# Layer 1, 64 dense tokens of block 1: high and low part of the acts as one operand of 128 columns in the output products

## The chip, the cores and the metric

One NeuronCore of a Trainium2 chip runs the whole program. The metric is the device time of one execution in microseconds, the median of some runs. A profile is one more execution, taken with the hardware profiler. Engines: PE (matrix products), DVE (VectorE), ACT (ScalarE), POOL (GpSimd, which issues the gathers) and SP (which issues the other transfers, in order).

## The reference, cut to what matters

A decoder trunk of two layers over 512 tokens of 1024 features. Each layer ends in a PEER mixer: eight heads choose 16 of 16,384 experts for each token, an expert being one row of `u_tab` and one of `v_tab`.

```python
        u = u_tab[e]
        a = jax.nn.gelu(jnp.einsum('pd,phkd->phk', xb, u).astype(jnp.float32), approximate=False)
        return jnp.einsum('phk,phkd->pd', g * a, v_tab[e].astype(jnp.float32)).astype(xb.dtype)
```

Here `e` are a token's 128 expert numbers, `g` their softmax weights, and the sum over them goes into the residual stream with a gate (`g2`).

## The kernel before, in words

The mixer is computed in two ways at once. For some tokens it is *sparse*: the chosen rows are gathered from DRAM, 128 rows of 1024 at a time (`gather_back`), and VectorE makes the dot products and the weighted sums. In layer 1 these are the 128 tokens of block 0 and the first 64 of block 1: 384 gathers, of which 96 come ahead of the dense steps. For the others it is *dense* (`dense`): all 16,384 experts are gone through in 128 steps of 128 experts, with a table of weights that is zero where a token did not choose an expert. In layer 1 these are 320 tokens, `T = 320`: the last 64 of block 1 (`LO[1] = 64`), and blocks 2 and 3, which in `dense` are b = 0, 1 and 2.

A dense step i has two products. The *act products* (L658) multiply a tile `u` of 128 experts with the 320 tokens' inputs into the PSUM tile `pa`; GELU and the weights `wg` make `g`, 128 experts by 320 tokens. The *output products* (L695) multiply `g`, as the stationary operand, with a tile `v` of 128 experts by 1024 features, and add into six PSUM banks `Y[b][h]`, three token blocks by two halves of 512 features. Operands are split into a high and a low part (float32r), `XH`, `XL` for `u` and `v`, `WH`, `WL` for `g`: ScalarE casts the high part (L246), VectorE subtracts for the low part (L247). A product is three matmuls: high by high, high by low, low by high. The first 28 steps' acts are made ahead (`NA = 28`, tile `ahead`), so steps 0 to 27 have output products only. In the program, step i+1's act products come ahead of step i's output products.

The order on each engine is set by the tile framework's scheduler, from priorities and its own estimate of durations; gathers' VectorE work is tied to steps by a list:

```python
PACE = [[1.5] * 28 + [2.5] * 100, [1.5] * 28 + [2.46] * 100]
```

So layer 1 takes 1.5 gathered tiles a step in steps 0 to 27 and 2.46 a step after. `u` and `v` share three buffers of 512 KB, gathered tiles four, and `wg` comes in ten loads of 256 KB for 16 steps, from the table that the kernel wrote to DRAM as `wd`.

After the last step `dense_end` multiplies `Y` with the gate row, adds the residual tiles `XD` and calls `final`, which normalizes and stores `out`. Its tiles (`XD`, `gate`, the norm's row `fg`, `fo`) are in a pool of their own, `fe`, opened when the dense pools are closed in the program's text; its memory is what those pools leave free, or free up. The tile `ahead` with its pad holds 28 x 320 x 4 + 768 = 36,608 bytes a partition until step 27 has read it. The `end` of the sparse part sums the two halves of the last gathered sum `y` (`go` brings the upper 64 partitions down), and does the same for its tokens with `gt`, `gx` and `gfg`.

Of the kernel before, what the change touches and what calls it, by code (L numbers as in the profile page):

```python
# [10 lines left out]
F32 = mybir.dt.float32  # L11
F32R = mybir.dt.float32r
# [4 lines left out]
ALU = mybir.AluOpType  # L17
# [3 lines left out]
P = 128  # L21
D = 1024
# [8 lines left out]
NK = 128  # L31
# [6 lines left out]
NBD = 3  # L38
# [3 lines left out]
LO = (0, 64)  # L42
# [9 lines left out]
def kernel(ctx, tc, x, c_col, pos, mod_w, mod_b, norm_g, w_in, w_gl, w_g2, b_g2, gla_ng, gla_wo,  # L52
                      kv_mod_w, kv_mod_b, kv_ng, kv_w, swa_wq, sinks, swa_wo, peer_wq, subk, peer_u, peer_v,
                      u_t, v_t, fin_g, out):
    nc = tc.nc
# [135 lines left out]
    def gated_add(env, X, half, y, gate, rows=slice(0, P)):  # L191
        t = env.tmp.tile([P, 512], F32, tag=env.t2k, name="ga")[rows]
        nc.vector.tensor_tensor(t, y[rows], gate[rows], op=ALU.mult)
        nc.vector.tensor_tensor(X[rows, ts(half, 512)], X[rows, ts(half, 512)], t, op=ALU.add)
# [50 lines left out]
    def split_rows(src, H, L, eng=nc.vector):  # L245
        cast = nc.scalar.copy(H, src)  # L246
        eng.tensor_tensor(L, src, H.bitcast(F32), op=ALU.subtract)  # L247
        return cast
# [351 lines left out]
    def dense(l, yps):  # L600
        Y = []
        first = []
        lastg = []
        outs = []
        lo = LO[l]
        T, G0 = TD - lo, lo // TG
# [5 lines left out]
        with tc.tile_pool(name="dna", bufs=1, reuse_waits="tile") as da, \  # L612
# [34 lines left out]
            def halves():  # L647
                return [dp.tile([P, D], F32R, tag=t, name=t, bufs=3) for t in ("XH", "XL")]

            def act(i, out, bank="pa"):  # L650
                u = dp.tile([P, KT, P], F32, tag="uv", name="u", bufs=3)
                nc.sync.dma_start(u, u_t[l, i])
                UH, UL = (t.rearrange("p (k t) -> p k t", t=P) for t in halves())
                split_rows(u, UH, UL)
                pa = psa.tile([P, 512], F32, tag=bank, name="pa")
                for n, (uu, hh) in enumerate(((UH, hH), (UH, hL), (UL, hH))):
                    for kt in range(KT):
                        nc.tensor.matmul(pa[:, :T], uu[:, kt, :], hh[:, kt, lo:], start=n + kt == 0,  # L658
                                         stop=n == 2 and kt == KT - 1)
                nc.scalar.activation(out, pa[:, :T], AF.Gelu)  # L660
# [8 lines left out]
            def stage1(i, wg):  # L669
                g = dp.tile([P, T], F32, tag="g", name="g")  # L670
                if i < NA:
                    src = ahead[:, i, :]
                else:
                    src = g
                    act(i, g)
                v = dp.tile([P, D], F32, tag="uv", name="v", bufs=3)
                nc.sync.dma_start(v, v_t[l, i])
                VH, VL = halves()
                split_rows(v, VH, VL)
                first.append(nc.vector.scalar_tensor_tensor(  # L680
                    g.rearrange("p (g t) -> p g t", t=TG), src.rearrange("p (g t) -> p g t", t=TG), 1.0 / GSC,
                    wg[:, :, ts(i % SL, TG)], op0=ALU.mult, op1=ALU.mult))
                WH = dp.tile([P, T], F32R, tag="WH", name="WH", bufs=2)
                WL = dp.tile([P, T], F32R, tag="WL", name="WL", bufs=2)
                lastg[:] = [split_rows(g, WH, WL)]
                return VH, VL, WH, WL

            def rows(b):
                return slice(0, P if b else P - lo)

            def stage2(i, VH, VL, WH, WL, blocks=range(NBD)):
                for b in blocks:
                    for a, vv in ((WH, VH), (WH, VL), (WL, VH)):
                        for h in range(2):
                            mm = nc.tensor.matmul(Y[b][h][rows(b), :], a[:, max(b * P - lo, 0):(b + 1) * P - lo], vv[:, ts(h, 512)],  # L695
                                                  start=i == 0 and a is WH and vv is VH,
                                                  stop=i == NK - 1 and a is WL)
                outs.append(mm)

            cur = slot(ds_)  # L700
# [16 lines left out]
            with tc.tile_pool(name="dnw", bufs=1, reuse_waits="tile") as dw:  # L717
                for k in range(parts):
                    slot_part(0, cur, k)
                Y += [[yps.tile([P, 512], F32, tag=f"y{2 * b + h}", name="Y") for h in range(2)] for b in range(NBD)]  # L720
                work = stage1(0, cur)
                for i in range(NK):
                    m, k = divmod(i, SL)
                    if k == 0 and i + SL < NK:
                        nxt = slot((dw, ds_)[m % 2])
                    if k < parts and i + SL < NK + k:
                        slot_part(m + 1, nxt, k)
                    if k == SL - 1:
                        cur = nxt
                    then = stage1(i + 1, cur) if i + 1 < NK else None  # L730
                    if i < NK - 2:
                        stage2(i, *work)
                    elif i == NK - 2:
                        for w, blocks in ((work, (0, 1)), (then, (0, 1)), (work, (2,)), (then, (2,))):
                            stage2(i + (w is then), *w, blocks)
                    work = then
        return Y, first, outs, lastg[0]

    def dense_end(fp, l, Y, X, after):
        gate = fp.tile([P, D], F32, tag="gate", name="gate")  # L740
        nc.sync.dma_start(gate, grow[l].partition_broadcast(P))
        for b in range(NBD):
            nc.sync.dma_start(X[b][:P if b else P - LO[l], :], xs[b + 1][0 if b else LO[l]:P, :])
        env = Env()
        env.tmp, env.t2k = fp, "t2k"
        for b in range(NBD):
            for h in range(2):
                gated_add(env, X[b], h, Y[b][h], gate[:, ts(h, 512)], slice(0, P if b else P - LO[l]))
            after(b)

    def preload_sqrt(pool, after):
# [241 lines left out]
    def swa_d(Y, yctx, mod, Ak, Bk, A, B, A4, B4, rbase, hT0, after, lastg):  # L993
        with ExitStack() as stack, tc.tile_pool(name="sd", bufs=1, reuse_waits="tile") as sp, \
# [34 lines left out]
            def after_add(b):  # L1029
                with tc.issue_after(first.ins):  # L1030
                    modulate_T(env, XD[b], (Ak, Bk, hk[b]), (A, B, hq[b]))

            dense_end(sp, 0, Y, XD, after_add)
            yctx.close()
            sps = stack.enter_context(tc.tile_pool(name="sdps", bufs=1, space=PSUM, reuse_waits="tile"))
# [153 lines left out]
    def ypool():  # L1189
        return tc.tile_pool(name="dnps", bufs=1, space=PSUM, reuse_waits="tile")  # L1190
# [5 lines left out]
    with prio(D0):  # L1196
        Y, at, outs, lastg = dense(0, yctx.enter_context(ypool()))
# [12 lines left out]
    with prio(D1):  # L1210
        Y, at, outs, lastg = dense(1, ctx.enter_context(ypool()))
        with prio(GG):
            gather_back(1, at, outs, *gs[1])
        with tc.tile_pool(name="fe", bufs=1, reuse_waits="tile") as fe:
            XD = xd_tiles(fe)
            fg = fe.tile([P, D], F32, tag="fg", name="fg")
            nc.sync.dma_start(fg, fin_g.partition_broadcast(P))
            env = Env()
            env.small = fe

            def final(b):
                o = fe.tile([P, D], F32, tag="fo", name="fo", bufs=2)
                lo = 0 if b else LO[1]
                q = slice(0, P - lo)
                r = rstd_of(env, XD[b][q, :], D, o[q, :], q)
                for h in range(2):
                    half = ts(h, 512)
                    nc.vector.scalar_tensor_tensor(o[q, half], XD[b][q, half], r, fg[q, half], op0=ALU.mult,
                                                   op1=ALU.mult)
                    nc.sync.dma_start(out[(b + 1) * P + lo:(b + 2) * P, half], o[q, half])  # L1230

            preload_sqrt(fe, lastg)
            dense_end(fe, 1, Y, XD, final)
# [67 lines left out]
```

## Time and profile before

| | us |
|---|---|
| median of 3 runs | 3237.35 (3230.11 to 3239.7) |
| the profiled execution's own time | 3229.43 |
| its span, first to last instruction | 3227.7 |
| PE, DVE, ACT busy | 2986.4, 2505.4, 1251.1 |
| layer 1's output products, first to last | 2312.5 to 3209.5 |

The span lies within the execution's time. Busy times are sums over the whole span, in which stages of different kinds follow each other; what a stage waits for is read in its own stretch. A PE row's length covers a matmul's whole way through the engine, so matmuls overlap in the rows: their pace is the distance between starts.

### The profile page before, as it was taken

The numbers are of one execution on the slowest core, as the hardware profiler recorded it, in microseconds if no ns is written. First come the engines' busy times: TensorE is split into PE (matmuls) and PEld (weight loads), VectorE is DVE, ScalarE is ACT, GpSimd is POOL, SyncE is SP. The second block draws the span as 40 slices with busy tenths as digits, with TensorE's granted clock in tenths as the row PEclk, the third lists the DMA queues.
The fourth block names the chain that finished last, engine by engine and source line by source line (L and its number), as shares of the span: only waits on it lengthen the run. The fifth ranks groups of instructions, "written<-read, shape, count | busy, mean of one in ns | idle before, by whom it ended". The sixth has DMA issues, their size and how long they took to land.

```text
span 3227.7 us, 45681 instructions
## 1 busy us (share of the span) xinstructions
PE 2986.4 (93%) x16674; PEld 2527.4 (78%) x16674; DVE 2505.4 (78%) x4879; ACT 1251.1 (39%) x1985; POOL 791.8 (25%) x669
## 2 busy tenths in 40 slices
PE   5999885999999999999999968789899999999997
PEld 4776685997999988999876535589678888878886
DVE  6865689978778777877653778889897877777888
ACT  3523323543333333333673332335433333433333
POOL 0000000025333433433000143320143333343332
PEclk9999998999999999999999979989899999999999
DMA  7678664889989999998634578877899899899987
GB/s 233 225 260 275 208 227 152 291 304 331 325 305 338 322 330 333 325 322 287 226 105 144 183 261 302 275 267 258 305 350 342 314 323 322 311 344 327 315 310 235
DMA packets 278970, 904.78 MB, mean 280 GB/s; under 512 B 29828, under 2 KB 75268, under 8 KB 273112
## 3 DMA queue, kind: packets, MB, share of 16 engines
q1 hardware_dynamic: 186584, 566.28, 49.8%
q0 software_dynamic: 92160, 335.59, 30.1%
q8 instruction: 130, 2.13, 0.3%
q14 instruction: 96, 0.79, 0.1%
HBM read 848.23 MB, written 52.96 MB: 279 GB/s over the span
## 4 chain that ended last, share of the span: by engine, by line
PE 58%; DMA 14%; DVE 12%; issue 10%; POOL 3%; ACT 2%; SPq 1%; POOLq 0%; DVEq 0%; ACTq 0%
PE Y L695 22%; PE pa L658 21%; PE ps_mm L545 4%; POOL gu L830 3%; DMA w<-in_peer_wq 3%; DMA u<-in_u_t 2%; DMA w<-in_mod_w 2%; PE pm L643 2%; DVE XL L247 2%; PE ps_m L1058 1%; DVE og L635 1%; DMA wg<-wd 1%; DMA gu<-in_peer_u,ei 1%; DVE gu L861 1%; DVE gacc L134 1%
## 5 line engine op out<-in xcount | busy, mean ns | idle before, releaser
L830 POOL DMA_INDIRECT gu<-in_peer_u,ei x256 | 324.2, 1266 | 1630.4 <-DVE gu L861 821.0
L247 DVE TENSOR_TENSOR XL<-u,XH 128x1024 fp32r<-128x1024 f32 x256 | 313.1, 1224 | 229.6 <-ACT XH L246 135.0
L695 PE MATMUL Y<-XH,WH 128*128 128x512 f32 (+1 forms) x1536 | 480.3, 393 | 11.4 <-ACT WH L246 11.4
L695 PE MATMUL Y<-XH,WL 128*128 128x512 f32 (+1 forms) x1536 | 477.3, 392 | 2.0 <-DVE WL L247 2.0
L695 PE MATMUL Y<-XL,WH 128*128 128x512 f32 (+1 forms) x1536 | 478.2, 392 | 0.1
L246 ACT CAST XH<-u 128x1024 fp32r<-128x1024 f32 x256 | 268.8, 1051 | 466.5 <-PE pa L658 233.1
L830 POOL DMA_INDIRECT gu<-in_peer_v,ei x256 | 315.9, 1234 | 517.1 <-DVE yg L873 458.3
L658 PE MATMUL pa<-hH,XH 128*128 128x384 f32 (+1 forms) x2048 | 380.6, 327 | 14.2 <-ACT g L660 12.4
L658 PE MATMUL pa<-hL,XH 128*128 128x384 f32 (+1 forms) x2048 | 377.8, 324 | 0.0
L658 PE MATMUL pa<-hH,XL 128*128 128x384 f32 (+1 forms) x2048 | 375.7, 323 | 2.2 <-DVE XL L247 2.2
L246 ACT CAST XH<-v 128x1024 fp32r<-128x1024 f32 x256 | 268.9, 1050 | 278.1 <-PE Y L695 240.2
L247 DVE TENSOR_TENSOR XL<-v,XH 128x1024 fp32r<-128x1024 f32 x256 | 312.8, 1222 | 73.5 <-ACT XH L246 72.0
L658 PEld LDWEIGHTS pa<-hH,XH 128*128 128x128 f32 x2048 | 340.5, 189 | 35.8 <-ACT g L660 18.0
L861 DVE SCALAR_TENSOR_TENSOR gu<-gu,htg 128x1024 f32<-128x1024 f32 x256 | 309.5, 1221 | 62.9 <-DMA gu<-in_peer_u,ei 62.5
L873 DVE SCALAR_TENSOR_TENSOR yg<-gu,a,yg 128x1024 f32<-128x1024 f32 x254 | 325.5, 1281 | 30.4 <-DMA gu<-in_peer_v,ei 28.9
L658 PEld LDWEIGHTS pa<-hL,XH 128*128 128x128 f32 x2048 | 337.8, 189 | 1.6 <-issue 0.8
L658 PEld LDWEIGHTS pa<-hH,XL 128*128 128x128 f32 x2048 | 335.3, 188 | 3.3 <-DVE XL L247 3.0
L695 PEld LDWEIGHTS Y<-XH,WL 128*128 128x128 f32 (+1 forms) x1536 | 275.0, 179 | 79.1 <-DVE WL L247 2.7
L695 PEld LDWEIGHTS Y<-XL,WH 128*128 128x128 f32 (+1 forms) x1536 | 275.3, 179 | 77.8 <-DVE XL L247 0.5
L695 PEld LDWEIGHTS Y<-XH,WH 128*128 128x128 f32 (+1 forms) x1536 | 274.1, 180 | 67.8 <-ACT WH L246 12.0
L246 ACT CAST WH<-g 128x384 fp32r<-128x384 f32 (+1 forms) x256 | 124.7, 487 | 456.8 <-DVE g L680 335.0
L545 PE MATMUL ps_mm<-hTd,w 128*128 128x128 f32 x1792 | 236.3, 291 | 32.1 <-DMA w<-in_peer_wq 27.0
(342 smaller groups left out, 3880.9 us busy)
## 6 DMA issues: line engine op xcount, KB each, us to landing
u<-in_u_t SPq DMA_DIRECT2D x256, 512.0 KB
v<-in_v_t SPq DMA_DIRECT2D x256, 512.0 KB
w<-in_peer_wq SPq DMA_DIRECT2D x128, 512.0 KB
w<-in_mod_w SPq DMA_DIRECT2D x96, 512.0 KB
wd<-wt SPq DMA_DIRECT2D x44, 1024.0 KB
wg<-wd SPq DMA_DIRECT2D x176, 256.0 KB
w<-in_gla_wo SPq DMA_DIRECT2D x32, 512.0 KB
w<-in_swa_wo SPq DMA_DIRECT2D x32, 512.0 KB
```

Of the source, the lines that this page charges most:

```text
L134: nc.vector.scalar_tensor_tensor(acc, w(kt), cs[:, kt:kt + 1], acc, op0=ALU.mult, op1=ALU.add)
L246: cast = nc.scalar.copy(H, src)
L247: eng.tensor_tensor(L, src, H.bitcast(F32), op=ALU.subtract)
L545: mm = nc.tensor.matmul(pq[:, ts(q, P)], w[:, kt, :], hT[:, kt, :], start=kt == 0, stop=kt == KT - 1)
L635: nc.vector.tensor_tensor(og[:, n], o2, wide(gn), op=ALU.mult)
L643: nc.tensor.matmul(pm[:, t, :], o1[:, u, :, w], og[:, n, u, :, w], start=n == 0, stop=n == 1)
L658: nc.tensor.matmul(pa[:, :T], uu[:, kt, :], hh[:, kt, lo:], start=n + kt == 0, stop=n == 2 and kt == KT - 1)
L695: mm = nc.tensor.matmul(Y[b][h][rows(b), :], a[:, max(b * P - lo, 0):(b + 1) * P - lo], vv[:, ts(h, 512)], start=i == 0 and a is WH and vv ...
L830: nc.gpsimd.indirect_dma_start(out=u, out_offset=None, in_=table, in_offset=bass.IndirectOffsetOnAxis(ap=e[:, i:i + 1], axis=0))
L861: nc.vector.scalar_tensor_tensor(u, u, 1.0, h, op0=ALU.mult, op1=ALU.mult, accum_out=a[:, i:i + 1])
L873: nc.vector.scalar_tensor_tensor(y, u, a[:, i:i + 1], y, op0=ALU.mult, op1=ALU.add)
L1058: nc.tensor.matmul(pqs[b], hTs[b][:, kt, :], w(kt), start=kt == 0, stop=kt == KT - 1)
```

## The change

Layer 1's block b = 0 has 64 tokens only. The high and low part of `g` now lie in one tile `W2` of 640 columns: 64 columns of low part of block 0, then 320 columns of high part, then the low part of the other two blocks. Its first 128 columns are block 0's low and high part side by side, and they are one stationary operand: with `VH` and with `VL`, two terms instead of three. The bank `Y[0][h]` then holds 64 rows of the low part's products and 64 rows of the high part's, which `dense_end` must add: it multiplies the whole bank with the gate into a tile `both`, has the upper 64 rows brought down by a transfer to a tile `low`, and adds both to `XD`. The blocks end in the order 1, 0, 2. In layer 0 (`LO = 0`) the tile is laid out anew, and the work is the same.

```diff
@@
-                WH = dp.tile([P, T], F32R, tag="WH", name="WH", bufs=2)
-                WL = dp.tile([P, T], F32R, tag="WL", name="WL", bufs=2)
-                lastg[:] = [split_rows(g, WH, WL)]
-                return VH, VL, WH, WL
-
-            def rows(b):
-                return slice(0, P if b else P - lo)
-
-            def stage2(i, VH, VL, WH, WL, blocks=range(NBD)):
+                W2 = dp.tile([P, 2 * T], F32R, tag="W2", name="W2", bufs=2)
+                n = T % P
+                H = W2[:, n:n + T]
+                lastg[:] = [nc.scalar.copy(H, g)]
+                for c in (slice(0, n), slice(n, T)):
+                    if c.stop > c.start:
+                        L = W2[:, 0:n] if n and not c.start else W2[:, n + T:]
+                        nc.vector.tensor_tensor(L, g[:, c], H[:, c].bitcast(F32), op=ALU.subtract)
+                return VH, VL, W2
+
+            def stage2(i, VH, VL, W2, blocks=range(NBD)):
+
                 for b in blocks:
-                    for a, vv in ((WH, VH), (WH, VL), (WL, VH)):
+                    if b or not lo:
+                        c = b * P - lo
+                        H, L = W2[:, T % P + c:][:, :P], W2[:, T + c:][:, :P]
+                        terms = (H, VH), (H, VL), (L, VH)
+                    else:
+                        both = W2[:, 0:P]
+                        terms = (both, VH), (both, VL)
+                    for n, (a, vv) in enumerate(terms):
                         for h in range(2):
-                            mm = nc.tensor.matmul(Y[b][h][rows(b), :], a[:, max(b * P - lo, 0):(b + 1) * P - lo], vv[:, ts(h, 512)],
-                                                  start=i == 0 and a is WH and vv is VH,
-                                                  stop=i == NK - 1 and a is WL)
+                            mm = nc.tensor.matmul(Y[b][h], a, vv[:, ts(h, 512)], start=i == 0 and n == 0,
+                                                  stop=i == NK - 1 and n == len(terms) - 1)
                 outs.append(mm)
@@
         env.tmp, env.t2k = fp, "t2k"
-        for b in range(NBD):
+        order = range(NBD)
+        if LO[l]:
+            both, low = (fp.tile([P, D], F32, tag=t, name=t) for t in ("both", "low"))
             for h in range(2):
-                gated_add(env, X[b], h, Y[b][h], gate[:, ts(h, 512)], slice(0, P if b else P - LO[l]))
+                nc.vector.tensor_tensor(both[:, ts(h, 512)], Y[0][h], gate[:, ts(h, 512)], op=ALU.mult)
+            nc.sync.dma_start(low[0:64, :], both[64:P, :])
+            nc.vector.tensor_tensor(X[0][0:64, :], X[0][0:64, :], both[0:64, :], op=ALU.add)
+            order = (1, 0, 2)
+        for b in order:
+            if LO[l] and b == 0:
+                nc.vector.tensor_tensor(X[0][0:64, :], X[0][0:64, :], low[0:64, :], op=ALU.add)
+            else:
+                for h in range(2):
+                    gated_add(env, X[b], h, Y[b][h], gate[:, ts(h, 512)])
             after(b)
```

On PE, in a step late in layer 1, from the end of the act products to the first products of block 1 (names are output, then moving and stationary operand; 64x512 or 128x512 is the output's shape), before:

```order
L658 MATMUL pa<-hH,XL 128x320 x8
L695 MATMUL Y<-XH,WH 64x512 x2
L695 MATMUL Y<-XL,WH 64x512 x2
L695 MATMUL Y<-XH,WL 64x512 x2
L695 MATMUL Y<-XH,WH 128x512 x2
```

And the whole step's output products with the change, `W_26376` being the tile `W2`:

```order
L658 MATMUL pa<-hH,XL 128x320 x8
L705 MATMUL Y<-XH,W_26376 128x512 x2
L705 MATMUL Y<-XL,W_26376 128x512 x2
L705 MATMUL Y<-XH,W_26376 128x512 x2
L705 MATMUL Y<-XL,W_26376 128x512 x2
L705 MATMUL Y<-XH,W_26376 128x512 x4
L705 MATMUL Y<-XL,W_26376 128x512 x2
L705 MATMUL Y<-XH,W_26376 128x512 x2
```

Block 0 has four products in place of six; blocks 1 and 2 have six each, as before.

On VectorE, one of the steps 28 to 127 (`y` with `gu` is a gathered tile's work, `XL` the low part of `v` or `u`, `WL` or `W` that of `g`), before:

```order
L247 TENSOR_TENSOR XL<-u,XH 128x1024
L680 SCALAR_TENSOR_TENSOR g<-g,wg 128x320
L873 SCALAR_TENSOR_TENSOR y_27903<-gu,a_27708,y_27903 128x1024
L247 TENSOR_TENSOR WL<-g,WH 128x320
L873 SCALAR_TENSOR_TENSOR y_27903<-gu,a_27708,y_27903 128x1024 x2
L247 TENSOR_TENSOR XL<-v,XH 128x1024
```

And with the change:

```order
L247 TENSOR_TENSOR XL<-u,XH 128x1024
L680 SCALAR_TENSOR_TENSOR g<-g,wg 128x320
L893 SCALAR_TENSOR_TENSOR y_27519<-gu,a_27324,y_27519 128x1024
L690 TENSOR_TENSOR W_26376<-g,W_26376 128x64
L690 TENSOR_TENSOR W_26376<-g,W_26376 128x256
L893 SCALAR_TENSOR_TENSOR y_27519<-gu,a_27324,y_27519 128x1024 x2
L247 TENSOR_TENSOR XL<-v,XH 128x1024
```

The subtraction is in two parts and stands at the same place of the step.

On the SP queue, before, about step 28, the loads for `dense_end` and `final` stand among those of `u` and `v`, and the end of the queue is short:

```order
L677 DMA v<-in_v_t 128x1024
L1217 DMA fg<-in_fin_g 128x1024
L741 DMA gate<-grow_109 128x1024
L652 DMA u<-in_u_t 128x1024
L743 DMA XD<-xs_111 64x1024
L677 DMA v<-in_v_t 128x1024
L743 DMA XD<-xs_112 128x1024
L652 DMA u<-in_u_t 128x1024
L743 DMA XD<-xs_113 128x1024
```

With the change, the end of the SP queue, behind the last load of `v`:

```order
L677 DMA v<-in_v_t 128x1024
L902 DMA go<-y_27519 64x1024
L859 DMA gt<-grow_109 128x1024
L1237 DMA fg<-in_fin_g 128x1024
L750 DMA gate<-grow_109 128x1024
L752 DMA XD<-xs_111 64x1024
L752 DMA XD<-xs_112 128x1024
L752 DMA XD<-xs_113 128x1024
L760 DMA low<-both 64x1024
L861 DMA gx<-xs_111 64x1024
L868 DMA gfg<-in_fin_g 128x1024
```

The five loads have moved from step 28 to behind `go`, which waits for `y`; the new transfer `low` stands behind them.

## Rows read from the trace of the kernel before

**Rows 1.** windows: busy us by engine, PE clock, DMA share, GB/s.
```profile
2312.50:2424.80 112.30, 112.30 (x486) 83.57 (x487) 102.64 (x156) 38.57 (x54) 51.49 (x42) 0.98 0.96 349
2420.00:2500.00 80.00, 77.52 (x423) 66.15 (x422) 60.15 (x64) 29.09 (x40) 31.40 (x23) 1.00 0.96 342
2500.00:3200.00 700.00, 691.13 (x3777) 597.68 (x3776) 555.68 (x651) 270.13 (x366) 256.35 (x222) 1.00 0.91 319
3209.00:3228.00 19.00, 0.51 (x3) 0.09 (x1) 14.39 (x23) 5.49 (x12) 0.00 (x0) 0.62 0.52 149
```

**Rows 2.** chain that ended last, 2300 to 3228 us, shares by line.
```profile
by line: PE Y L695 45.4%; PE pa L658 32.7%; DMA u<-in_u_t 6.1%; issue 4.1%; DMA wg<-wd 3.9%; DMA gu<-in_peer_u,e 1.4%; SPq L664 1.1%; DVE XL L247 1.0%; DVE yg L873 0.8%; ACT XH L246 0.4%; DVE WL L247 0.3%; DVE gu L861 0.3%; DVE fo L1228 0.3
```

**Rows 3.** pieces of that chain: start us, length us, what.
```profile
2583.85 13.07 DMA u<-in_u_t
...
2957.02 4.12 PE Y L695 x18
2961.14 3.51 PE pa L658 x24
2964.66 4.12 PE Y L695 x18
```

**Rows 4.** timeline of PE in one step: start us, length us, instruction.
```profile
3003.12 0.62 PE L695 MATMUL Y<-XL,WH 128*64 128x512 f32 x2
...
3003.36 0.36 PEld L695 LDWEIGHTS Y<-XH,WL 128*64 128x64 f32 x2
3003.58 0.62 PE L695 MATMUL Y<-XH,WL 128*64 128x512 f32 x2
...
3004.04 0.63 PE L695 MATMUL Y<-XH,WH 128*128 128x512 f32 x2
3004.28 0.42 PEld L695 LDWEIGHTS Y<-XL,WH 128*128 128x128 f32 x2
...
3004.50 0.63 PE L695 MATMUL Y<-XL,WH 128*128 128x512 f32 x2
```

**Rows 5.** DVE groups, 2412-3209 us: count, busy us, mean ns, idle.
```profile
L247 DVE TENSOR_TENSOR XL<-v,XH 128x1024 fp32r<-128x1024 f32 x103 | 125.9, 1223 | 34.0 <-ACT XH L246 32.7 <-issue 1.3
...
L247 DVE TENSOR_TENSOR XL<-u,XH 128x1024 fp32r<-128x1024 f32 x100 | 122.5, 1225 | 120.7 <-ACT XH L246 74.2 <-PE pa L658 46.5
...
L247 DVE TENSOR_TENSOR WL<-g,WH 128x320 fp32r<-128x320 f32 x103 | 50.3, 488 | 0.0
```

**Rows 6.** DMA issues, 2412 to 3209 us: count, KB each.
```profile
u<-in_u_t SPq DMA_DIRECT2D x100, 512.0 KB
v<-in_v_t SPq DMA_DIRECT2D x100, 512.0 KB
wg<-wd SPq DMA_DIRECT2D x50, 256.0 KB
```

**Rows 7.** timeline of the SP queue around the end of the first 28 steps.
```profile
2419.12 0.33 SPq L1217 DMA_DIRECT2D fg<-in_fin_g  x1
2419.50 0.42 SPq L741 DMA_DIRECT2D gate<-grow  x1
...
2427.81 0.47 SPq L743 DMA_DIRECT2D XD<-xs  x1
```

**Rows 8.** timeline of the last 22 us.
```profile
3206.43 0.47 SPq L882 DMA_DIRECT2D go<-y  x1
...
3208.89 0.61 PE L695 MATMUL Y<-XH,WL 128*128 128x512 f32 x2
...
3209.32 0.69 DVE L193 TENSOR_TENSOR ga<-Y,gate 128x512 f32<-128x512 f32 x1
3209.93 1.21 DVE L883 TENSOR_TENSOR y<-y,go 64x1024 f32<-64x1024 f32 x1
...
3222.48 1.42 DVE L1228 SCALAR_TENSOR_TENSOR fo<-XD,rs,fg 128x512 f32<-128x512 f32 x2
3223.29 0.96 SPq L1230 DMA_DIRECT2D out<-fo  x2
```

## The prediction

> **What bounds the kernel now.** I read the windows first, to part layer 1's dense work into its stages; then the chain of work that ended last, for what each stage waits on; then the timeline of one step, the VectorE groups, and the tail.
>
> The change touches layer 1's output products, so only the time after 2300 us counts. There the reader is to see that 45.4% of the chain is the output products (L695) and 32.7% the act products (L658), while transfers of `u` and `wg` hold 10.0% together [rows 2]. In the steady part a step of the chain is 3.51 us of act products (24 matmuls) and 4.12 us of output products (18 matmuls), one right behind the other, 7.63 us a step [rows 3]. Three stages have different covers:
>
> - Steps 0 to 27 (2312 to 2425 us) have no act products, those were made ahead. PE is full (112.30 of 112.30 us), but so is nearly everything else: VectorE 102.64 us, DMA share 0.96 at 349 GB/s [rows 1].
> - Steps 28 to 127. Between 2500 and 3200 us PE is busy 691.13 of 700 us, so 8.9 us are lost; VectorE is at 79%, DMA at 0.91 and 319 GB/s [rows 1]. PE bounds this stage, and DMA is close behind.
> - The tail, 3209 to 3228 us: PE is done and VectorE is busy 14.39 of 19 us [rows 1].
>
> **The change part by part.** *Output products.* Block 0 had three terms by two halves with 64 columns of acts, and has two terms by two halves with 128: six matmuls become four, 18 become 16 in a step. Does a matmul with a stationary operand of 128 columns cost more than one with 64? The rows say no: two matmuls with 64 columns start at 3003.12 and the next two at 3003.58, two with 128 at 3004.04 and 3004.50: 0.46 us a pair in both cases, 0.23 us each, and the weight loads (0.36 and 0.42 us a pair) lie beside the matmuls before them [rows 4]. So a step loses 2 x 0.229 = 0.458 us of PE: 7.63 becomes 7.17. Were nothing else in the way, 128 steps would give 58.6 us.
>
> *Steps 28 to 127: up to 45.8 us.* What is late next is DMA. A step moves `u` 0.524 MB, `v` 0.524 MB [rows 6], 0.164 MB of `wg` (ten loads of 256 KB for 16 steps) and 2.46 gathered tiles of 0.524 MB (the pace list), 2.50 MB in all. In 7.63 us that is 328 GB/s, in 7.17 us 349 GB/s. The first stage shows 349 GB/s held for 112 us without PE waiting [rows 1], so the mean just fits, but the `wg` loads come in clumps (2.62 MB within some five steps): five steps then want 5 x 2.34 + 2.62 = 14.3 MB, 41.0 us at 349 GB/s, against 38.2 us of PE before and 35.9 after. Before, the 8.9 us lost between 2500 and 3200 us lie at such places (the 13.07 us for `u` at 2584 is one) [rows 1, 3]. The shortfall grows by 2.3 us at each of the five to six clumps, 13 us. I take 45.8 - 13 = 33 us. The bounds: 0 if DMA gives no more than today's 328 GB/s, 45.8 if it gives all that is asked.
>
> *Steps 0 to 27: up to 12.4 us.* DMA already moves 349 GB/s there, and VectorE gets one instruction more (below): (102.64 + 4.2) / 27 = 3.96 us a step against PE's new 3.66. So at most 0.16 us a step is left by VectorE and next to nothing by DMA. I take 2 us, bounds 0 and 4.
>
> *VectorE's low part.* One subtraction of 320 columns becomes two, of 64 and 256. 320 columns take 488 ns and 1024 take 1223 ns [rows 5]: 1.044 ns a column and 154 ns fixed. So 221 + 421 = 642 ns, 154 ns more a step. In steps 28 to 127 it lies in idle time: VectorE does 555.68 us of work in 700 us, 6.06 us a step [rows 1], 6.21 after, below 7.17. The Trainium skill ("Perfetto Trace Analysis", section Optimizing Scalar/DVE Operations) gives about 60 ns of fixed engine time for an instruction on SBUF; by it the split would cost 0.06 us a step, not 0.154. The sum stays as it is, and the price in the slower rival would be less than half. The trace's slope decides here. The block-0 product now waits for the small subtraction too, where it waited for ScalarE's cast only; that subtraction stands a whole act product ahead of its use, so nothing is late.
>
> *Loads that move to the end.* This is in the order of the SP queue and not in the diff's words. The two new tiles (8 KB a partition) bring the closing pool from about 30.7 to 38.9 KB, more than the 36.6 KB that the tile of early acts leaves free. So `fg`, `gate` and the three `XD` (2.36 MB) are no longer loaded at 2419 to 2428 us [rows 7] but behind `go`, which waits for the last gathered sum. At 2420 to 2500 us DMA runs at 342 GB/s, and PE misses 2.5 us there [rows 1]; 2.36 MB less is 6.9 us of DMA. I take 3 us of gain, bounds 0 and 7.
>
> *The tail.* `go` is issued at 3206.43 us [rows 8], some 0.15 us later after the change. Ahead of VectorE's first new product stand `go`, `gt`, `fg` and `gate`, 1.83 MB, 5.3 us at 349 GB/s, and a fixed time: `go`, itself 0.75 us of transfer, was used at 3209.93, 3.5 us after its issue at the latest, so at most 2.75 us. I take 2.2 us: `gate` lands at 3214.1, in the old time scale. Behind it VectorE has before's 14.39 us, less the two 1.21 us operations on `y` that now come earlier, plus two products of 0.69 us and two additions of 1.21 us: 15.8 us, and it ends at 3229.9 where it ended at 3223.9 [rows 1, 8]. The ScalarE passes now stand in another order behind these; I give them 2 us. So the tail is 8 us longer. The bounds are 4 (no fixed time, no ScalarE wait) and 14 (the whole 3.1 MB from `go` to the last `XD` lands before anything can start). The 0.9 us that PE saves in its last two steps is inside that wait.
>
> *Sum:* -33 - 2 - 3 + 8 = -30 us. The profiled execution took 3229.4 us, so 3199; it stood 7.9 us under the median of the runs shown, 3237.35. I carry the difference over: **3207 us**. With all bounds at once: -45.8 - 4 - 7 + 4 = -53, and +14.
>
> **The rivals.**
>
> *PE stays the only bound.* DMA serves the faster steps, clumps included. For it: 349 GB/s is just what is wanted, and the share there was 0.96, not 1. The Trainium skill ("DMA: Bandwidth & Descriptors", section Where 436 GB/s comes from) puts the limit of a core's HBM transfers at about 358 GB/s, which would allow this; no stage of this trace holds 358. Against it: PE waits at clumps already. -45.8 - 2 - 5 + 8 = -45: 3192 us.
>
> *DMA is the bound already.* Steps 28 to 127 stay at 7.63 us, since gathers and loads together get no more than 328 GB/s in this mix, and the time saved on PE turns into waits for `u` and `wg`. For it: the 10% of the chain [rows 2]. Against it: 349 GB/s in the first stage, with the gathers among it. Gain from the moved loads 6 us, tail +8: +2, 3239 us.
>
> *Slower: VectorE's queue is the loop.* It works in order, and in each step its two subtractions on `v` and `u` wait, 34.0 + 120.7 us over 103 steps, 1.5 us a step [rows 5]. With 6.06 us of work that is 7.56 us, nearly the step itself. If those waits don't shrink with PE's step (the casts ahead of them wait for buffers), the 0.154 us is added to each step: 100 x 0.154 = 15 us, and with the tail's 8 us +23: 3260 us. It decides from the point where work and waits together pass 7.63 us. Against it: the waits end on PE or on a cast that waits for PE, so they should give way.
>
> *It doesn't do what it says:* only if a 128-column load stood in the way of its matmul, which rows 4 deny.
>
> **How the numbers follow.** Forecast 0.50, PE alone 0.22, DMA bound already 0.18, VectorE 0.10. 0.3% of 3237 is 9.7 us, about what a measurement can tell here from no change: faster means under 3227.6. The forecast spreads some 12 us to each side and is faster in nearly all of that; the third case falls mostly in the middle. So faster 0.76, same 0.15, slower 0.09. The range must reach the second rival and most of the third: 3182 to 3237. The forecast's own is 3195 to 3220.
>
> **What would show it.** Right: 16 output products in 3.66 us a step in the chain, steps of 7.2 us with longer waits for `u` and `wg` at the clumps, DMA near 340 GB/s; steps 0 to 27 as long as before; `fg`, `gate` and `XD` issued behind `go`, and VectorE idle some 2 to 3 us for `gate` at the end, with a tail of about 27 us from PE's last matmul. Wrong: steps still of 7.6 us with DMA below 335 GB/s, VectorE without idle time in steps 28 to 127, or a tail over 32 us.

## The result and the profile after

The changed kernel takes **3210.31 us** (median of 4 runs, 3199.2 to 3210.71), the kernel before in the same comparison 3238.52 us (4 runs, 3230.11 to 3248.27). By these medians that is 28 us less, where 30 were forecast. The ratio on record, 0.9896 with the 95% interval [0.9879, 0.9913], is not the ratio of the medians and stands for 28 to 39 us. A second comparison gave 0.9874 [0.9845, 0.9903].

To see where the time went I cut layer 1's dense work at the starts and ends of PE instructions: stage 1 from the first output product to the first act product (27 steps' output products), stage 2 from there to the last output product (100 steps' act products, 101 steps' output products), and the tail to the end of the span. "Lost" is stage 2 less its pure PE time, which is 100 x 3.51 + 101 x 4.12 = 767.1 us before [rows 3] and 100 x 3.52 + 101 x 3.65 = 720.7 us after (chain below). It holds the time without a matmul and what matmuls took beyond their pure time.

| profile | stage 1 | stage 2 | lost | tail | sum |
|---|---|---|---|---|---|
| before | 112.37 | 784.64 | 17.5 | 18.20 | 915.21 |
| after | 109.20 | 746.81 | 26.2 | 27.53 | 883.54 |
| after, second profile (again) | 108.32 | 752.50 | 31.9 | 27.47 | 888.29 |

The sum falls by 31.7 us (26.9 by the second profile). The span falls by 19.0 us only, from 3227.7 to 3208.7, because what lies ahead of the first output product, where the two kernels do the same work, took 2325.16 us in this execution and 2312.49 in the one before. So the stages are compared, and the spans are not.

Windows of the changed kernel: stage 1, stage 2, and the last 29 us (busy us by engine in the order PE, weight loads, VectorE, ScalarE, GpSimd, then PE clock, DMA share, GB/s):
```profile
2325.16:2434.36 109.20, 102.97 (x433) 82.21 (x433) 100.28 (x183) 38.51 (x54) 53.77 (x40) 0.98 0.95 344
2434.36:3181.17 746.81, 729.70 (x4017) 661.36 (x4015) 623.76 (x817) 297.81 (x407) 328.81 (x245) 0.99 0.93 333
3180.00:3209.00 29.00, 1.17 (x6) 0.63 (x4) 17.96 (x26) 5.45 (x12) 0.00 (x0) 0.57 0.67 199
```
PE was full in stage 1 and is no longer: 6.2 us of 109.20 are idle. DMA moves 333 GB/s in stage 2, against 319 in most of it before [rows 1]. The end has 17.96 us of VectorE work in 29 us, before 14.39 in 19.

What stage 2 lost has two parts. In 746.81 - 729.70 = 17.1 us PE had no matmul, and its matmuls took 729.70 - 720.7 = 9.0 us more than their pure time. Stage 2 before, then the three stretches of the changed kernel's stage 2 in which the granted clock was at the lower of its two levels (0.50, 1.2 GHz), and an act product in the first of them:
```profile
2424.86:3209.50 784.64, 773.29 (x4219) 667.28 (x4217) 619.20 (x719) 300.39 (x408) 284.10 (x243) 1.00 0.90 318
...
2487.61:2494.44 6.83, 5.93 (x22) 5.93 (x23) 6.25 (x8) 3.30 (x5) 2.54 (x2) 0.50 0.65 211
2726.54:2733.37 6.83, 5.47 (x20) 5.47 (x21) 5.62 (x7) 3.51 (x5) 2.08 (x2) 0.50 0.59 190
2842.60:2849.42 6.82, 4.98 (x19) 4.99 (x20) 5.34 (x9) 2.89 (x4) 1.70 (x2) 0.50 1.06 384
...
2488.51 6.44 PE pa L658 x24
```
Each stretch began during one of the stage's three longest waits (3.83, 3.66 and 6.31 us) and went on into the matmuls behind it; the act product took 6.44 us in place of 3.52. The wait of 2.72 us shown below was followed by no such stretch. Before, the stage was 11.4 us without a matmul and 6.2 us over its pure time, with 6.8 us at the lower clock. So a long wait can cost more than the wait itself here.

The chain that ended last, from 2330 us to the end, shares by line:
```profile
by line: PE Y L705 34.4%; PE pa L658 33.4%; DMA u<-in_u_t 10.3%; issue 3.7%; DMA v<-in_v_t 3.3%; DVE XL L247 2.7%; DMA gu<-in_peer_u,e 1.8%; DVE gu L881 1.7%; DMA gu<-in_peer_u,ei 1.0%; DVE W L690 0.9%; DMA gate<-grow 0.8%; ACT XH L246 0.7%
```
The output products are down from 45.4% to 34.4%, and transfers of `u` have risen from 6.1% to 10.3% [rows 2].

Pieces of that chain around one clump of `wg` loads (start us, length us, what):
```profile
2573.79 3.65 PE Y L705 x16
2577.44 3.52 PE pa L658 x24
2580.95 3.65 PE Y L705 x16
...
2589.22 10.93 DMA u<-in_u_t
...
2601.66 3.78 PE pa L658 x24
```
A step is 3.65 us of output products (16 matmuls) and 3.52 us of act products, 7.17 us, where it was 7.63 [rows 3]. Then the chain leaves PE for a transfer of `u` of 10.93 us. That isn't all PE's loss; PE's own timeline there says how much is:
```profile
2598.32 0.61 PE L705 MATMUL Y<-XH,W 128*128 128x512 f32 x2
2601.66 1.43 PE L658 MATMUL pa<-hH,XH 128*128 128x320 f32 x8 [2.72 <-ACT g L660]
```
PE had work for most of the transfer and then idled 2.72 us. The releaser named, `g` at L660, is the GELU of the act product before. On ScalarE it stands behind the cast of the late `u`:
```profile
2600.23 1.04 ACT L246 CAST XH<-u 128x1024 fp32r<-128x1024 f32 x1 [7.37 <-DMA u<-in_u_t]
2601.18 0.43 ACT L660 ACTIVATE g<-pa 128x320 f32<-128x320 f32 x1
```
ScalarE itself had waited 7.37 us for that `u`, so the transfer is what came late.

What the SP queue issued there (start us, length us, instruction):
```profile
2580.63 0.33 SPq L652 DMA_DIRECT2D u<-in_u_t  x1
2583.51 0.33 SPq L677 DMA_DIRECT2D v<-in_v_t  x1
2583.91 3.10 SPq L664 DMA_DIRECT2D wg<-wd  x6
2589.22 0.34 SPq L652 DMA_DIRECT2D u<-in_u_t  x1
2590.36 0.58 SPq L677 DMA_DIRECT2D v<-in_v_t  x1
2590.99 1.76 SPq L664 DMA_DIRECT2D wg<-wd  x3
2596.42 0.34 SPq L652 DMA_DIRECT2D u<-in_u_t  x1
2596.80 0.58 SPq L664 DMA_DIRECT2D wg<-wd  x1
```
The ten `wg` loads of the next slot go out within 13 us, six of them in one piece ahead of the late `u`. In this stretch the DMA engines are full (share 1.04), at 394 GB/s, a higher rate than in any whole stage here:
```profile
2582.00:2602.00 20.00, 17.28 (x94) 15.21 (x93) 13.23 (x16) 6.35 (x10) 7.53 (x5) 1.00 1.04 394
```

PE in one step's output products of block 0 (start us, length us, instruction):
```profile
3001.51 0.63 PE L705 MATMUL Y<-XH,W 128*128 128x512 f32 x2
3001.98 0.62 PE L705 MATMUL Y<-XL,W 128*128 128x512 f32 x2
3002.44 0.62 PE L705 MATMUL Y<-XH,W 128*128 128x512 f32 x2
```
A pair with 128 columns starts 0.46 to 0.47 us after the pair before it, as before [rows 4].

VectorE's groups between 2500 and 3170 us (count, busy us, mean ns, idle before and its releasers):
```profile
L247 DVE TENSOR_TENSOR XL<-u,XH 128x1024 fp32r<-128x1024 f32 x91 | 111.5, 1225 | 90.3 <-ACT XH L246 69.9 <-PE pa L658 18.3 <-PE Y L705 1.3
L247 DVE TENSOR_TENSOR XL<-v,XH 128x1024 fp32r<-128x1024 f32 x91 | 111.1, 1220 | 4.5 <-ACT XH L246 4.2
...
L690 DVE TENSOR_TENSOR W<-g,W 128x256 fp32r<-128x256 f32 x91 | 37.9, 417 | 0.0
L690 DVE TENSOR_TENSOR W<-g,W 128x64 fp32r<-128x64 f32 x91 | 19.8, 217 | 0.0
```
The low part is two instructions of 217 + 417 = 634 ns, 146 ns more than the one of 488 [rows 5]. But VectorE's rows overlap as PE's do, and what an instruction costs the queue is the distance of starts. One step before and one with the change:
```profile
3000.40 0.49 DVE L247 TENSOR_TENSOR WL<-g,WH 128x320 fp32r<-128x320 f32 x1
3000.80 1.22 DVE L861 SCALAR_TENSOR_TENSOR gu<-gu,h 128x1024 f32<-128x1024 f32 x1
...
3007.44 0.56 DVE L690 TENSOR_TENSOR W<-g,W 128x64 fp32r<-128x64 f32 x2
3007.91 1.28 DVE L893 SCALAR_TENSOR_TENSOR y<-gu,a,y 128x1024 f32<-128x1024 f32 x1
```
The one subtraction holds VectorE 0.40 us and the two together 0.47 (in the median 402 ns against 136 + 335), so the split costs 0.07 us a step. The waits ahead of the two other subtractions went down from 1.5 to (90.3 + 4.5) / 91 = 1.04 us a step.

The tail, VectorE (start us, length us, instruction, idle before and its releaser):
```profile
3181.94 1.22 DVE L903 TENSOR_TENSOR y<-y,go 64x1024 f32<-64x1024 f32 x1 [3.03 <-DMA go<-y]
3183.68 1.22 DVE L862 TENSOR_TENSOR y<-y,gt 64x1024 f32<-64x1024 f32 x1 [0.52 <-DMA gt<-grow]
3187.47 1.29 DVE L759 TENSOR_TENSOR both<-Y,gate 128x512 f32<-128x512 f32 x2 [2.58 <-DMA gate<-grow]
...
3201.47 0.15 DVE L155 RECIPROCAL rs<-sd 64x1 f32<-64x1 f32 x1 [1.12 <-ACT sd L153]
...
3203.05 1.41 DVE L1248 SCALAR_TENSOR_TENSOR fo<-XD,rs,fg 128x512 f32<-128x512 f32 x2
```
and the SP queue:
```profile
3178.94 0.47 SPq L902 DMA_DIRECT2D go<-y  x1
3179.50 0.54 SPq L859 DMA_DIRECT2D gt<-grow  x1
3180.08 0.62 SPq L1237 DMA_DIRECT2D fg<-in_fin_g  x1
3180.76 0.43 SPq L750 DMA_DIRECT2D gate<-grow  x1
3181.23 1.69 SPq L752 DMA_DIRECT2D XD<-xs  x3
```
`fg`, `gate` and `XD`, issued at the end of the first 28 steps before [rows 7], are now issued behind `go` [rows 8]. VectorE waits 2.58 us for `gate`, and its product starts 8.5 us after the issue of `go`.

### The profile page after: what moved, and what is told of

The parts are those of the page before. It is cut to its first block, busy times and chain, and to the rows that moved or that the text cites. A ratio compares the mean times of both kernels' runs of the same rounds, so it can differ in the third digit from the quotient of the medians.

```text
span 3208.7 us, 45233 instructions
## 1 busy us (share of the span) xinstructions
PE 2937.3 (92%) x16418; PEld 2516.9 (78%) x16418; DVE 2510.7 (78%) x5007; ACT 1248.3 (39%) x1985; POOL 839.4 (26%) x669
## 4 chain that ended last, share of the span: by engine, by line
PE 55%; DMA 16%; DVE 12%; issue 11%; POOL 4%; ACT 2%; SPq 0%; POOLq 0%; DVEq 0%; ACTq 0%
PE pa L658 20%; PE Y L705 17%; PE ps_mm L545 4%; DMA u<-in_u_t 4%; POOL gu L850 4%; DMA w<-in_peer_wq 3%; PE pm L643 2%; DMA gu<-in_peer_v,ei 2%; DVE XL L247 2%; DMA v<-in_v_t 2%; PE ps_m L1078 1%; DVE gu L881 1%; PE ps_mm L264 1%; PE ps_mm L265 1%; PE ps_mm L263 1%
## 5 line engine op out<-in xcount | busy, mean ns | idle before, releaser
L705 PE MATMUL Y<-XH,W 128*128 128x512 f32 x2816 | 810.1, 393 | 19.9 <-ACT W L686 11.7
L705 PEld LDWEIGHTS Y<-XH,W 128*128 128x128 f32 x2816 | 523.2, 188 | 123.0 <-DVE W L690 13.0
L705 PE MATMUL Y<-XL,W 128*128 128x512 f32 x1536 | 477.6, 392 | 0.1
L850 POOL DMA_INDIRECT gu<-in_peer_v,ei x256 | 339.7, 1327 | 481.2 <-DVE yg L893 254.4
L705 PEld LDWEIGHTS Y<-XL,W 128*128 128x128 f32 x1536 | 289.1, 188 | 64.2 <-DVE XL L247 0.6
L686 ACT CAST W<-g 128x384 fp32r<-128x384 f32 (+1 forms) x256 | 124.8, 487 | 413.4 <-DVE g L680 340.9
L545 PEld LDWEIGHTS ps_mm<-hTd,w 128*128 128x128 f32 x1792 | 221.1, 202 | 45.5 <-DMA w<-in_peer_wq 33.7
L690 DVE TENSOR_TENSOR W<-g,W 128x384 fp32r<-128x384 f32 (+2 forms) x384 | 141.6, 396 | 14.7 <-ACT W L686 14.5
```

What stands on the lines that cost most here:

```text
L545: mm = nc.tensor.matmul(pq[:, ts(q, P)], w[:, kt, :], hT[:, kt, :], start=kt == 0, stop=kt == KT - 1)
L686: lastg[:] = [nc.scalar.copy(H, g)]
L690: nc.vector.tensor_tensor(L, g[:, c], H[:, c].bitcast(F32), op=ALU.subtract)
L705: mm = nc.tensor.matmul(Y[b][h], a, vv[:, ts(h, 512)], start=i == 0 and n == 0, stop=i == NK - 1 and n == len(terms) - 1)
L850: nc.gpsimd.indirect_dma_start(out=u, out_offset=None, in_=table, in_offset=bass.IndirectOffsetOnAxis(ap=e[:, i:i + 1], axis=0))
```

## The experiments

Two theories stood after the result. One: what kept the 45.8 us of PE in stage 2 from being had in full is transfers that are late behind the `wg` clumps. The other: it is VectorE, with its one instruction more in a queue worked in order. Beside them, three terms of the sum could be tried alone: the matmuls, the split, and the tail.

**again.** The changed kernel once more, beside the kernels below.

> The changed kernel once more, beside the next three on one chip. Theory (PE's saved time, cut by waits for transfers, less a longer tail): 0.99 of the time before; from the first output product of layer 1 to its first act product some 109 us, from there to the last output product some 747 us, and 27.5 us from there to the end. What lies ahead of layer 1's dense steps should differ from run to run by some 10 us without any change in the code, since the two profiles do.

Measured: 3202.34 us, ratio 0.9874 [0.9845, 0.9903]. Its stages stand in the table above; stage 2 is 5.5 us longer than expected, and the work ahead took 20.55 us less than in the first profile, where some 10 were expected. The 5.7 us in stage 2 between two executions of one kernel is the size below which a single profile of a stage decides nothing here.

**e1_tail_fits.** The product of the upper 64 rows goes into a tile that is there, so that the closing pool fits and the five loads go back to the end of the first 28 steps.

```diff
-            both, low = (fp.tile([P, D], F32, tag=t, name=t) for t in ("both", "low"))
+            low = fp.tile([P, D], F32, tag="low", name="low")
             for h in range(2):
-                nc.vector.tensor_tensor(both[:, ts(h, 512)], Y[0][h], gate[:, ts(h, 512)], op=ALU.mult)
-            nc.sync.dma_start(low[0:64, :], both[64:P, :])
+                nc.vector.tensor_tensor(X[0][64:P, ts(h, 512)], Y[0][h][64:P], gate[64:P, ts(h, 512)], op=ALU.mult)
+            nc.sync.dma_start(low[0:64, :], X[0][64:P, :])
...
+            for h in range(2):
+                gated_add(env, X[0], h, Y[0][h], gate[:, ts(h, 512)], slice(0, 64))
```

> The tile both is left out: the upper 64 rows' product goes into the unused half of XD's first tile, so the closing pool is 4 KB a partition smaller and its five loads stand at step 28 again. Theory (the late loads make the tail): 19 to 21 us from the last output product to the end instead of 27.5, and 2 to 4 us more around step 28, together 3 to 6 us less than the changed kernel. Rival (the tail is long because two halves of block 0 must be added across partitions): the tail stays at 25 us or more and the time at that of the changed kernel.

Measured: 3207.89 us, ratio 0.9882 [0.9855, 0.9909]; stage 1 107.48, stage 2 755.01, tail 21.14 us. The tail gives back 6.4 of its 9.3 us, so the five late loads are most of its growth, and 18.20 to 21.14, about 3 us, is the price of the extra products and additions. The five loads do stand at the end of the first 28 steps again, at 2426.80 to 2436 us. The 3 to 6 us that were expected for the whole did not come: it isn't faster than the changed kernel, and stage 2 is 2.5 to 8.2 us longer than in its two profiles.

**e2_third_term.** Block 0 gets its third term back, as a repeated second one; layout, split and tail stay as changed.

```diff
-                        terms = (both, VH), (both, VL)
+                        terms = (both, VH), (both, VL), (both, VL)
```

> Block 0 gets its second term twice, so PE has 18 output products a step again, with layout, split subtraction and tail as changed; the output counts the low part of v twice for these tokens. Theory (all of the gain is PE's): steps of 7.63 us, some 780 us from the first act product to the last output product, and 5 to 10 us more than the kernel before, since the longer tail is left alone. Rival (the gain is the 2.4 MB of loads that left step 28): at most 10 us more than the changed kernel, still 15 us under the kernel before.

Measured: 3246.11 us, ratio 1.0011 [0.999, 1.0032]; stage 1 114.40, the tail 26.70. Its stage 2:
```profile
2435.38:3220.70 785.32, 771.70 (x4219) 695.97 (x4217) 623.69 (x815) 301.82 (x407) 293.99 (x243) 0.99 0.89 316
```
It takes 785.32 us, before it was 784.64. So the whole gain is the two matmuls, and in stage 2 neither the 128-column operand nor the split costs anything that shows. Stage 1 is 2.0 us longer than before, which one profile can't settle. The run also shows nothing of the 3 us that the loads taken out of stage 2 should give.

**e3_split_in_three.** The low part in three subtractions (64 + 128 + 128 columns).

```diff
-                for c in (slice(0, n), slice(n, T)):
+                for c in (slice(0, n), slice(n, n + P), slice(n + P, T)) if n else (slice(0, T),):
...
```

> The low part of the acts is taken in three subtractions (64, 128, 128 columns), 0.15 us more of VectorE in each step. Theory (VectorE has idle time in steps 28 to 127): at most 4 us more than the changed kernel, all of it in steps 0 to 27, where VectorE is nearly full (109 to 113 us). Rival (VectorE's queue is the loop): 0.15 us in each of 128 steps, 19 us more than the changed kernel, 15 of them after step 27.

Measured: 3207.06 us, ratio 0.9875 [0.9849, 0.9901]; stage 1 106.45, stage 2 751.95. Both lie within those of the changed kernel's two profiles or below them, so one more instruction a step shows no loss. It is a weak test, though: by the distance of starts the third subtraction costs 0.07 us a step (2 x 202 ns against 335), 7 us in stage 2 and not the 15 of the rival, while the two profiles of one kernel differ by 5.7. That VectorE's queue is not the loop is decided by e4_no_wg and e5_spread.

**e4_no_wg.** Layer 1 uses the first slot's weights for every step.

```diff
...
-                    if k == 0 and i + SL < NK:
-                        nxt = slot((dw, ds_)[m % 2])
...
+                    if not l:
+                        if k == 0 and i + SL < NK:
+                            nxt = slot((dw, ds_)[m % 2])
...
```

> Edit: the changed kernel, but layer 1 loads only the first of its wg slots and uses its weights for every step; the other wg loads of layer 1, which come in clumps, are left out, so the output products of the later steps take the wrong slices. The instruction stream of TensorE and VectorE stays. Theory (after the change the time that TensorE loses in steps 28 to 127, 13.3 us of 670 in the profile after, is transfers that come late behind the wg clumps): those losses go, steps 28 to 127 take 728 to 738 us instead of 746.8 to 752.5, and steps 0 to 27, where the DMA engines are .96 busy, come down from 109 to 95 to 104 us; the whole 3180 to 3192, ratio to the kernel before 0.982 to 0.985. Rival (the losses are VectorE's order of splits, or gaps of TensorE's own): steps 28 to 127 stay within 2 us of 747 to 752, the whole within 0.3% of the changed kernel.

Measured: 3178.66 us, ratio 0.9804 [0.9789, 0.9819]; stage 1 101.28, stage 2 724.68, of which 4.0 us lost:
```profile
2424.31:3148.99 724.68, 721.81 (x4017) 654.22 (x4015) 623.69 (x817) 297.06 (x407) 334.60 (x245) 1.00 0.91 325
```
The rival falls: with the same work on VectorE (623.69 us, in the changed kernel 623.76) the losses go. The gain is a little larger than the theory's upper end.

Its chain by line between 2440 and 3160 us:
```profile
by line: PE Y L705 43.1%; PE pa L658 42.4%; DMA u<-in_u_t 2.9%; issue 2.5%; DMA gu<-in_peer_u,e 2.4%; POOL gu L853 1.1%; DVE XL L247 1.0%; DMA gate<-grow 0.9%; DVE gu L884 0.7%; DMA out<-gfo 0.6%; DVE y L896 0.4%; DVE XD L194 0.2%; DVE ga L
```
Two products in equal parts, and little else.

**e5_spread.** The same bytes, but the ten `wg` loads of a slot one by one behind `v` loads.

```diff
...
+                vloads.append(nc.sync.dma_start(v, v_t[l, i]))
...
-                    if k < parts and i + SL < NK + k:
+                    spread = (0, 1, 3, 4, 6, 7, 9, 10, 12, 13)
+                    if l and k in spread and i + SL < NK + k:
+                        with tc.issue_after(vloads[-1].ins):
+                            slot_part(m + 1, nxt, spread.index(k))
+                    elif not l and k < parts and i + SL < NK + k:
...
```

> Edit: the changed kernel with layer 1's wg loads not in a clump of ten but one behind every v load, at ten of the sixteen steps of a slot. The bytes stay the same. Theory (the clump makes the u and v behind it late, and the DMA engines have room over a whole slot: .94 busy and 337 GB/s in steps 28 to 127): steps 28 to 127 take 735 to 745 us, ratio to the kernel before 0.983 to 0.987. Rival (the DMA engines have no room left, so that the order of loads only moves the wait): steps 28 to 127 stay at 746 to 753, ratio 0.987 to 0.990. A loss, ratio over 0.991, would say that the spread loads come too late for the slot that needs them.

Measured: 3183.81 us, ratio 0.9821 [0.98, 0.9842]. Windows of stage 1 and stage 2:
```profile
2327.89:2430.64 102.75, 102.04 (x433) 82.11 (x434) 100.10 (x183) 38.51 (x54) 53.67 (x40) 0.98 0.98 363
2430.64:3160.05 729.41, 722.72 (x4017) 654.01 (x4015) 622.07 (x817) 292.82 (x407) 336.03 (x245) 1.00 0.94 341
```
Stage 1 takes 102.75 us, stage 2 729.41 with 8.8 lost, against 26.2 and 31.9, and the granted clock stays at its upper level through stage 2 (1.00): the order of the loads alone, with no byte less, gives back 17 to 23 us in stage 2 and 6 in stage 1. It is more than expected. Its chain by line between 2440 and 3160 us:
```profile
by line: PE Y L706 33.5%; PE pa L659 33.4%; DMA u<-in_u_t 13.0%; issue 4.5%; DVE XL L247 3.6%; DVE gu L886 1.9%; ACT XH L246 1.5%; POOL gu L855 1.3%; DMA gu<-in_peer_u,e 1.2%; DVE y L898 1.2%; DMA gu<-in_peer_v,ei 1.1%; DMA gate<-grow 0.9%;
```
The reader is to see that `u` has 13.0% of this chain, more than in the changed kernel, though PE loses only 8.8 us. As at 2589 us above, the chain goes along a transfer while PE still has work; where both take nearly the same time in a step, a share of DMA in the chain is not time that PE lost. The stage less its pure PE time is.

**e6_spread_tail.** e1_tail_fits and e5_spread together.

> Edit: e1_tail_fits (the upper rows' product written into a tile that is there, so that the five late loads fit at step 28 again) with the wg loads spread as in e5_spread. Theory: the two edits add: the tail 21 us instead of 27.5 and steps 28 to 127 in 738 to 748 us, 3 to 12 us less than the changed kernel, ratio to the kernel before 0.983 to 0.987. Rival: the five loads that come back at step 28 take DMA time that the spread would have given, as in e1_tail_fits: the time is that of the changed kernel, 0.987 to 0.989.

Measured: **3176.99 us** (5 runs, 3169.31 to 3184.99), ratio 0.9796 [0.9781, 0.9811], against 3239.9 of the kernel before on the same chip. Windows of stage 1 and stage 2:
```profile
2327.85:2429.41 101.56, 100.88 (x433) 81.82 (x433) 99.50 (x180) 38.28 (x54) 50.25 (x40) 0.98 0.98 368
2429.41:3162.00 732.59, 725.63 (x4017) 656.91 (x4015) 623.55 (x823) 291.63 (x407) 344.17 (x245) 1.00 0.95 343
```
Stage 1 101.56, stage 2 732.59, tail 21.30 us. This is more than expected. Against e5_spread the tail gives 6.25 us. Stage 2 is 3.2 us longer and stage 1 1.2 us shorter, less than the 5.7 us between two executions of one kernel, so what the five loads cost at step 28 is not shown. It is the fastest kernel of the study, 63 us under the kernel before, though its interval and e5_spread's touch.

**e7_before_spread.** The kernel before, with 18 output products, and its `wg` loads spread in the same way.

> Edit: the kernel before (18 output products, low part apart) with the wg loads spread as in e5_spread. Theory: in the kernel before TensorE loses 8.9 us of 700 in steps 28 to 127, so the spread can give at most 9 us there: ratio 0.997 to 1.000. If it gave more than it does to the changed kernel, the clumps would not be what the change ran into.

Measured: 3226.84 us (10 runs), ratio 0.9957 [0.9939, 0.9975]; stage 1 112.34, stage 2 773.64:
```profile
2432.91:3206.55 773.64, 770.10 (x4219) 666.20 (x4217) 619.97 (x719) 303.13 (x408) 272.66 (x242) 1.00 0.91 323
```
It gives 11.0 us in stage 2, more than the 9 that I had put as the most: I had counted idle time of PE between 2500 and 3200 us, but the stage begins at 2425 and lost 17.5 us in all. In stage 1 it gives nothing, since PE is full there [rows 1].

So the clumps cost 17.5 - 6.5 = 11.0 us of stage 2 before the change, and 26.2 (or 31.9) - 8.8 = 17.4 to 23.1 after it. Of the 17.4, 10.4 are time without a matmul and 7.0 are slower matmuls.

## Why the prediction was right, and where a term was off

- **16 output products for 18: right.** A step is 7.17 us, and with 18 again (e2_third_term) stage 2 is as long as before.
- **The clumps take a part of it: right in mechanism, and near in size partly by luck.** The forecast had the shortfall grow by 13 us. It grew by 6.4 to 12.1 us by the spread kernels, and stage 2's losses by 8.7 or 14.4 in the two profiles. Stage 2 fell by 37.8 (or 32.1) us; forecast were 33, and 3 for the loads that left it. The working behind the 13 us was off in three places. The ten loads go out within 13 us, in two steps and not five. The DMA engines move 394 GB/s there, where I had 349 for the ceiling. And the fall of PE's clock in the long waits has no term in the sum.
- **"I take 3 us of gain" for the moved loads: not settled.** e6_spread_tail against e5_spread shows 3.2 us and e1_tail_fits against the changed kernel 2.5 to 8.2, but e2_third_term against before shows none. Single profiles of a stage differ by 5.7 us, so the term can't be told apart.
- **Steps 0 to 27: the size was near, its reason wrong.** Forecast were 2 us, measured 3.2 to 4.1. I held 349 GB/s for what DMA can give there, and VectorE's 3.96 us a step for the floor; neither was one. With the loads spread the same 27 steps took 102.75 and 101.56 us, 3.8 us a step, at 363 and 368 GB/s. The 349 GB/s of before was what a full PE asked for, no limit. What kept the changed kernel at 109 us was the clumps here too: without them or with them spread stage 1 took 101.28 to 102.75 us, in the four profiles of 16 products with the clumps 106.45 to 109.20. In e6_spread_tail PE is full again, 100.88 of 101.56 us, so most of the 12.4 us can be had. VectorE is close behind with 99.50 us. Stage 1 of the changed kernel holds 100.28 us of its work, not the 106.8 that I got by adding 4.2 to 102.64; the split's part of that is 27 x 0.07 = 1.9 us.
- **The split on VectorE: hidden, as forecast, but at less than half the price.** I read 154 ns fixed off the rows' lengths, and by lengths the split is 146 ns. The rows overlap: by the distance of starts it costs VectorE 69 ns a step (136 + 335 against 402). Over the 100 steps of stage 2 VectorE's work went from 619.20 to 623.76 us, 0.05 us a step and not 0.15. The Trainium skill ("Perfetto Trace Analysis", section Optimizing Scalar/DVE Operations) gives about 60 ns of fixed engine time for an instruction on SBUF, and says that the profiled latency is about twice that because its second half overlaps with the next instruction. The trace agrees roughly, with 69 ns by the starts and some 150 ns in the rows. So the slope of the rows' lengths, which I let decide, was the wrong reading.
- **The tail: right, +9.3 for +8.** `gate` was ready 8.5 us after the issue of `go`, where 7.5 were forecast; the five late loads cost 6.4 us (e1_tail_fits) and the extra work some 3.
- **The rivals.** "PE stays the only bound" had the right rate and the wrong order: DMA does serve the faster step (e5_spread), but not with the loads in clumps. The 358 GB/s that it names as a limit was passed over whole stretches, with 363 (e5_spread) and 368 GB/s (e6_spread_tail). "DMA is the bound already" falls with the step of 7.17 us at 333 GB/s in the mean of stage 2. "VectorE's queue" falls with e4_no_wg and e5_spread, where PE goes faster with the same work on VectorE, and with the waits that shrank from 1.5 to 1.04 us a step. Its price of 15 us was too high by the same misreading of the rows. What spoke against it held in part: the waits end on casts, those of `v` wait for PE, but those of `u` now wait for `u`'s transfer in 129.8 of 179.3 us (2500 to 3170 us).
- **The carry to the median** was partly luck. The profiled execution before stood 9 us under the median of its comparison, the one after stood at its median, 3210.38 us, where the sum gave 3199. The 7.9 us that I carried over did not show as such; the work ahead of the change, which is common to both, took 12.7 us more in the second execution, and that took their place.

## What to carry to other kernels

When the engine that bounds a step is made faster, look at the order of the loads and not at the mean rate alone: here the mean fitted, and 24 us more (of 883.54) sat behind ten loads issued together, in part because PE's clock fell in the waits. A rate measured where another engine sets the pace is what was asked for, not what can be had. Where rows overlap, as VectorE's do here, an instruction's price is read from the distance of starts and not from its row's length. And a new tile of a few KB may move loads that no line of the diff names; it can be made to fit by writing into a tile whose contents aren't needed yet.

## What the runs showed that I had not expected

- The work ahead of layer 1's dense steps, the same products in all the kernels profiled, ended between 2304.61 us (again) and 2327.89 us (e5_spread), and 20.55 us apart in two executions of one kernel. That is not much less than the change gives. In these two executions PE was busy 2093.00 and 2104.59 us there, at the lower clock for 151 and 182 us. Whether the clock is the cause or follows from other waits is not shown.
- The DMA engines moved 368 GB/s over 101.56 us at a share of 0.98 (e6_spread_tail, gathers among it), where the most seen in a stage before was 349; at a clump of the changed kernel it was 394 over 20 us.
